# Decoder block on one core: where the first value group is split, and where the weights behind a pair's last cover step are prepared

## The chip, the core and the metric

The kernel runs on one core of a Trainium2 chip. The core has a matrix engine (TensorE, PE in the profile), a vector engine (VectorE, DVE), a scalar engine (ScalarE, ACT), a general one (GpSimd, POOL) and a queue that issues transfers (SyncE, SP). Each engine works through its own list of instructions in order and waits for the others by semaphores. The metric is the device time of one execution in microseconds (us).

## The reference, cut to what matters

The block mixes tokens in two branches, chunked retention and dilated sliding-window attention, merges them with gates and adds an MLP. The change lies in the attention branch and the gate projections beside it:

```python
for gi, (win, dil) in enumerate(ATT_GROUPS):          # 3 groups, 4 heads each
    aq, ak, av = parts[4 + 3 * gi], parts[5 + 3 * gi], parts[6 + 3 * gi]
    o, lse = dilated_group(heads(aq, 4), heads(ak, 4), heads(av, 4), tab, win, dil)
    outs.append(o)
    lses.append(lse)
o_all = jnp.stack(outs, axis=0)
wts = jax.nn.softmax(jnp.stack(lses, axis=0), axis=0)     # weights of the three groups
att = jnp.einsum('gbhs,gbhsd->bshd', wts, o_all).reshape(B, S, ATT_GROUP_W)
att_out = att @ w_att_out
merged = jax.nn.sigmoid(gate_a) * ret_out + jax.nn.sigmoid(gate_b) * att_out
```

Inside `dilated_group` the scores get a bias, a maximum per row, an exponential and a sum; the probabilities then multiply the values.

## The kernel before, in words

**Products in three parts.** Float32 operands are split into a high half (a copy to the rounded type, on ACT) and a low half (a subtraction, on DVE). `mm3` (line 198) makes a product of three matmuls: low weight by high data (L201), high by low (L203), high by high (L205). The products with the values do the same in `pv_mm` (L1399 to L1401), with `pth`/`ptl` the halves of the transposed probabilities and `vh`/`vl` those of the values. A weight's split is `split_w` (L191 on ACT, L192 on DVE).

**Steps.** The program is a list of steps (class `Steps`, line 55), each with loads and a body. A load goes through a ring of three raw tiles on SP's queue (L85): when one is used, the next in the list is issued. For a step that isn't marked `manual` the runner prepares weights of the next one or two steps before its body; a `manual` step gets a function (`ahead`, here `args[0]`) and calls it where it wants the next step's weights prepared, with a bound on how many.

**Attention.** The heads are treated in two pairs (`pair` 0 and 1). Each pair has six attention steps (`att_step`), one for each of three groups and two heads, which project keys and, woven into them, compute the scores of the head before. Then come cover steps (`cover_step`), whose gate projections (8 groups of matmuls, tile `gate`) fill PE while softmax and the products with the values go on:

- The last attention step issues the loads of the first group's values (`v_fetch(pair, 0)`, L1286).
- Cover step 0 weaves in the last scores, then `scores_end` (maximum L1250/L1251 and `ng` L1260 on DVE; eight exponentials, each with its sum, on ACT, L1263), `weights` (the softmax over the groups, L1333 to L1350, with one small exponential L1337 on ACT) and `pscale(0, a)` (L1358 on DVE, L1360 on ACT). At its end ACT takes the gate's sigmoid (L1529), which frees the PSUM bank of the gate; there are two such banks, shared by the gates and the sums of the value products.
- Cover step 1 splits the first group's values, `v_split(pair, 0)`: two copies (L1292, `vh`) and two subtractions (L1293, `vl`).
- Cover step 2 multiplies group 0 (`weave_pv(..., pair, 0)`): transposes (L1375), `pth`/`ptl` (L1379/L1380), products, and `pv_end`, which takes the sum out of PSUM (L1408 on ACT for group 0, L1412 on DVE for the others). Within it the values of group 1 are split, and behind it group 1 is scaled.
- Pair 0 has a cover step 3, which multiplies group 1 and scales group 2 within. Its group 2 is multiplied in the first attention step of pair 1, which also splits that group's values. Pair 1 has cover steps 0 to 2, and its groups 1 and 2 are multiplied in `gate_step`, behind which the output projection (`att_out_step`, tile `ao`) follows.

ACT's and DVE's order is the order of these calls. Cover step 2 is `manual`; cover step 3 and the gate step aren't, so two weight splits (`raw_8615`/`raw_8724` in pair 0, `raw_9954`/`raw_10063` in pair 1) stand at the start of each.

Of the kernel before, what the change touches and what calls it, by code (L numbers as in the profile page):

```python
# [20 lines left out]
NK = D // P  # L21
# [12 lines left out]
COVER = ((0, 1, 2, 3), (4, 5, 6), (9,))  # L34
# [100 lines left out]
def block_kernel(ctx, tc, io, stop=None, dbg=None):  # L135
    nc = tc.nc
    ctx.enter_context(tc.manual_schedule())

    def fv(t):
        return t.bitcast(F32)  # L140
# [44 lines left out]
    steps = Steps(nc, wraw, 3)  # L185
# [300 lines left out]
    def at(gen, n, call):  # L486

        for i, _ in enumerate(gen):
            if i == n:
                call()  # L490
            yield

    def drain(gen):
        for _ in gen:
            pass
# [238 lines left out]
    def wsplit(ap):  # L734
        return ap, split_w
# [373 lines left out]
    for h in range(H):  # L1109
        for c in range(NC):  # L1110
            steps.add((lambda h, c: lambda ahead, *w: chunk(h, c, ahead, *w))(h, c),
                      ([wsplit(io["w_rg"][4 * h + c // 2])] if c % 2 == 0 else []) + [mod_load(later_mods[8 * h + c])],
                      manual=True)


    A = {}
# [14 lines left out]
    def pslice(g, t, blk):  # L1131

        if g == 0:
            return (t[:, 0:128], 1) if blk == 0 else (t[:, 128 + 256 * (blk - 1):128 + 256 * blk], 2)
        if g == 1:
            r, n = blk // 2, blk % 2
            return (t[:, 384 * r:384 * r + 128], 1) if n == 0 else (t[:, 384 * r + 128:384 * r + 384], 2)
        return t[:, 128 * blk:128 * (blk + 1)], 1
# [108 lines left out]
    def scores_end(pair, g, a):  # L1247
        p, t, st = A["p"], A["P", g, a], A["st"]
        if g == 0:
            nc.vector.reduce_max(st[:, g, 0:1, a], t[:, 0:128], axis=AX.X)  # L1250
            nc.vector.reduce_max(st[:, g, 1:8, a], t[:, 128:].rearrange("p (b x) -> p b x", b=7), axis=AX.X)  # L1251
        elif g == 1:
            tv = t.rearrange("p (r x) -> p r x", r=4)
            sv = st[:, g].rearrange("p (r n) x -> p r n x", n=2)
            nc.vector.reduce_max(sv[:, :, 0, a], tv[:, :, 0:128], axis=AX.X)
            nc.vector.reduce_max(sv[:, :, 1, a], tv[:, :, 128:384], axis=AX.X)
        else:
            nc.vector.reduce_max(st[:, g, :, a], t.rearrange("p (b x) -> p b x", b=8), axis=AX.X)
        ng = p.tile([P, 8], F32, tag="ng", bufs=2, name=f"ng{pair}{g}{a}")
        nc.vector.tensor_scalar_mul(ng, st[:, g, :, a], -1.0)  # L1260
        for blk in range(8):
            v = pslice(g, t, blk)[0]
            nc.scalar.activation(v, v, AF.Exp, bias=ng[:, blk:blk + 1], accum_out=st[:, g, blk, 2 + a:3 + a])  # L1263
# [13 lines left out]
    def v_tile(pair, g, j, n):  # L1277
        if g == 0:
            return A["r1"].tile([P, S], F32R, tag="att", bufs=8, name=f"{n}{pair}{g}{j}")
        return ring(f"{n}{pair}{g}{j}")  # L1280
# [4 lines left out]
            lo = A["l", g, j] = v_tile(pair, g, j, "vl")  # L1285
            nc.sync.dma_start(fv(lo).rearrange("p (a b) -> p a b", a=4), v_rows(pair, g, j))  # L1286

    def v_split(pair, g):
        for j in range(2):
            lo = A["l", g, j]  # L1290
            hi = v_tile(pair, g, j, "vh")
            nc.scalar.copy(hi, fv(lo))  # L1292
            nc.vector.tensor_sub(lo, fv(lo), fv(hi))  # L1293
            A["v", g, j] = (hi, lo)

    def vblk(g, blk, a, i):
        j, b = (blk % 2, blk // 2) if g == 1 else (blk // 4, blk % 4)
# [14 lines left out]
    def blocks(t, g):  # L1312

        return t.rearrange("p (r n) x -> p r n x", n=2) if g == 1 else t
# [9 lines left out]
    def weights(pair):  # L1324

        p, st = A["p"], A["st"]
        stn = [st[:, 0], A["stn"][:, 1], A["stn"][:, 2]]
        mx = p.tile([P, 8, 2], F32, tag="mx", name=f"mx{pair}")
        wt = p.tile([P, 3, 8, 2], F32, tag="wt", name=f"wt{pair}")
        pr = p.tile([P, 3, 8, 2], F32, tag="pr", name=f"pr{pair}")  # L1330
        sm = p.tile([P, 8, 2], F32, tag="ssum", name=f"ssum{pair}")
        wg = p.tile([P, 2, 8, 2], F32, tag="wg", name=f"wg{pair}")
        nc.vector.tensor_max(mx, stn[0][:, :, 0:2], stn[1][:, :, 0:2])  # L1333
        nc.vector.tensor_max(mx, mx, stn[2][:, :, 0:2])
        for g in range(3):
            nc.vector.tensor_sub(wt[:, g], stn[g][:, :, 0:2], mx)
        nc.scalar.activation(wt, wt, AF.Exp)  # L1337
        for g in range(3):
            nc.vector.tensor_mul(pr[:, g], wt[:, g], stn[g][:, :, 2:4])
        nc.vector.tensor_add(sm, pr[:, 0], pr[:, 1])  # L1340
        nc.vector.tensor_add(sm, sm, pr[:, 2])
        nc.vector.reciprocal(sm, sm)
        for g in range(3):
            nc.vector.tensor_mul(wt[:, g], wt[:, g], sm)
        A["w", 0] = wt[:, 0]
        ds = [dram.tile([S, 2], F32, name=f"wtd{pair}{g}") for g in (1, 2)]
        for g in (1, 2):
            nc.sync.dma_start(natural(ds[g - 1], 0, 2), wt[:, g])
        for g in (1, 2):
            nc.sync.dma_start(blocks(wg[:, g - 1], g), natural(ds[g - 1], g, 2))  # L1350
            A["w", g] = wg[:, g - 1]

    def pscale(g, a):
        t, w = A["P", g, a], A["w", g]
        for blk in range(8):
            v = pslice(g, t, blk)[0]
            if blk in (0, 2, 4, 5, 7):
                nc.vector.tensor_scalar_mul(v, v, w[:, blk, a:a + 1])  # L1358
            else:
                nc.scalar.mul(v, v, w[:, blk, a:a + 1])  # L1360
        A["scaled", g, a] = True
# [85 lines left out]
    def weave_pv(main, n, pair, *groups):  # L1447


        parts, waits = sum(4 * len(PT[g]) for g in groups), 2 * len(groups) + 1  # L1450
        heavy = max(1.0, (parts - waits) / max(1, n - waits))
        total = parts + waits * (heavy - 1)
        done = share = 0
        for wait in pv(pair, *groups):
            share += heavy if wait else 1
            while done * total < share * n:
                next(main, None)
                done += 1
        drain(main)
# [38 lines left out]
    def cover_step(pair, n):  # L1498


        i = COVER[pair][n]

        def body(*args):
            ps = ps_mm(f"gate0{i}")
            gen = proj_gen(ps, args[-1])
            if n == 0:
                v_fetch(pair, 1)
                weave(gen, 6, scores_gen(pair, *combos[-1]), len(SB[0]), lag=2, rest=False)
                drain(gen)
                scores_end(pair, *combos[-1])  # L1510
                weights(pair)
                for a in range(2):
                    pscale(0, a)
            elif n == 1:
                drain(at(gen, 4, lambda: v_split(pair, 0)))
            elif n == 2:
                v_fetch(pair, 2)

                gen = at(gen, 3, lambda: (args[0](3), v_split(pair, 1)))
                weave_pv(gen, NK - 1, pair, 0)  # L1520
                for a in range(2):
                    pscale(1, a)
            else:
                weave_pv(at(gen, 3, lambda: [pscale(2, a) for a in range(2)]), NK - 1, pair, 1)
            if n > 1:
                t = A["r1"].tile([P, S], F32, tag="att", bufs=8, name=f"g0{i}s")
            else:
                t = ring(f"g0{i}s", F32)
            nc.scalar.activation(t, flat(ps), AF.Sigmoid)  # L1529
            nc.sync.dma_start(gate_d[i], t)  # L1530
        return body

    for pair in range(2):
        for i, (g, a) in enumerate(combos):
            steps.add(att_step(pair, i),
                      [wsplit(io["w_ak"][g * 4 + 2 * pair + a])] +
                      ([(aq_d[pair, *combos[i - 1]], q_prep(pair, *combos[i - 1]))] if i > 0 else []),
                      manual=i == pair == 0)
        for n in range(len(COVER[pair])):
            more = [(aq_d[pair, *combos[-1]], q_prep(pair, *combos[-1]))] if n == 0 else []  # L1540
            steps.add(cover_step(pair, n), more + [wsplit(io["w_gate"][len(COVER[0]) * pair + n])], manual=n == 2)


    G = {}
    gate_ctx = ExitStack()
    mh_ctx = ExitStack()

    def gate_step(w):

        ps = ps_mm("gate9")  # L1550
        gen = at(proj_gen(ps, w), 2, lambda: v_split(1, 2))
        gen = at(gen, 3, lambda: [pscale(2, a) for a in range(2)])
        weave_pv(gen, NK - 1, 1, 1, 2)
        att_ctx.close()
        G["p"] = gate_ctx.enter_context(tc.tile_pool(name="gates", bufs=1, side="right", reuse_waits="tile"))
        t = G["p"].tile([P, S], F32, tag="g1", bufs=8, name="g11")
        nc.scalar.activation(t, flat(ps), AF.Sigmoid)
        G[1, 1] = t
        for j in (0, 2, 3):
            gate_load(1, j)  # L1560
        open_mh()
# [3 lines left out]
        G[b, j] = G["p"].tile([P, S], F32, tag=f"g{b}", bufs=8, name=f"g{b}{j}")  # L1565
        nc.sync.dma_start(G[b, j], gate_d[8 * b + j])

    steps.add(gate_step, [wsplit(io["w_gate"][len(COVER[0] + COVER[1])])])

    def open_mh():  # L1570
        hpool_ctx.close()
# [878 lines left out]
```

## Time and profile before

| what | us |
|---|---|
| median of three runs | 2247.46 |
| lowest and highest run | 2244.88, 2249.23 |
| the profiled execution, its own time | 2244.46 |
| its span, first to last instruction | 2242.7 |
| pair 0: cover step 0 begins on PE | 1061.1 |
| pair 0: cover step 2 / cover step 3 begin on PE | 1087.2 / 1109.0 |
| pair 1: cover step 2 / gate step begin on PE | 1245.6 / 1267.4 |
| output projection begins on PE | 1298.2 |

The mean granted clock of PE is 0.995 of full speed. In the lines of the profile, `L1292 ACT CAST vh<-vl` is a copy by ACT from tile `vl` to tile `vh` at line 1292; a bracket behind a line of the timeline tells how long the engine was idle before it and what released it. `x2` is two such instructions merged. Tile numbers such as `raw_8615l` are the program's own: `h` and `l` behind them are the halves. SPq is SP's queue, where the time is that of issuing and not of the transfer.

### The profile page before, as it was taken

To read this page: it belongs to the slowest core of one execution; us is meant where nothing else is said; L and a number is where in the kernel's file an instruction comes from. 1 tells how busy PE (TensorE), PEld (TensorE's weight loads), DVE (VectorE), ACT (ScalarE), POOL (GpSimd) and SP (SyncE) were. 2 spreads that over 40 slices of the span, in tenths; PEclk is the share of its full clock that TensorE was granted. 3 is DMA by queue.
4 is the path that set the end of the run, shared out by engine and by line. 5 is a ranking of instruction groups with operands and counts; after the bars stand their busy time and mean duration, and the time that the engine had idled before them with its cause. 6 is when DMAs were issued, how large, how long until landed. Compare 5 with 4: busy or idle time off the path is not lost.

```text
span 2242.7 us, 27133 instructions
## 1 busy us (share of the span) xinstructions
PE 2182.0 (97%) x10130; PEld 1804.8 (80%) x10130; DVE 1454.8 (65%) x2285; ACT 908.4 (41%) x1665; POOL 145.4 (6%) x168
## 2 busy tenths in 40 slices
PE   7999999999999999999999999999999999999998
PEld 5887888887877888888888788888777777888887
DVE  6527777754548778855555654677866665787845
ACT  4323333223334445544634633524444444533412
POOL 0001111000011122110000000002000000000003
PEclk9999999999999999999999999999999999999999
DMA  9548999624775556549723365654243344745322
GB/s 362 198 146 279 284 294 277 202 95 178 251 269 167 168 181 208 192 161 247 226 66 97 96 223 180 238 182 153 75 149 138 141 155 148 268 147 169 122 85 76
DMA packets 154371, 408.93 MB, mean 182 GB/s; under 512 B 27062, under 2 KB 54973, under 8 KB 149822
## 3 DMA queue, kind: packets, MB, share of 16 engines
q1 hardware_dynamic: 148542, 363.14, 46.5%
q0 software_dynamic: 5696, 44.04, 8.3%
q8 instruction: 80, 1.31, 0.2%
q14 instruction: 53, 0.43, 0.1%
HBM read 316.27 MB, written 156.13 MB: 211 GB/s over the span
## 4 chain that ended last, share of the span: by engine, by line
PE 44%; DVE 8%; ACT 4%; issue 2%; DMA 1%; POOL 0%; SPq 0%; POOLq 0%; DVEq 0%; ACTq 0%
PE fp L201 2%; PE fp L203 2%; PE fp L205 2%; PE f2a L203 2%; PE f2a L201 2%; PE f2a L205 2%; PE ak L201 2%; PE ak L203 2%; PE ak L205 2%; PE wo L201 1%; PE wo L203 1%; PE wo L205 1%; PE roa L205 1%; PE roa L203 1%; PE roa L201 1%
## 5 line engine op out<-in xcount | busy, mean ns | idle before, releaser
L201 PE MATMUL qap<-hh,qaw 128*128 128x512 f32 x216 | 84.3, 390 | 3.4 <-DVE qat L285 1.7
L205 PE MATMUL qap<-hh,qaw 128*128 128x512 f32 x216 | 84.1, 389 | 0.0
L203 PE MATMUL qap<-hl,qaw 128*128 128x512 f32 x216 | 84.1, 389 | 0.0
L611 POOL TENSOR_TENSOR j<-qk,j 128x512 fp32r<-128x512 f32 x32 | 43.3, 1354 | 469.8 <-ACT j L610 469.8
L1909 ACT ACTIVATE a<-a 128x512 f32<-128x512 f32 x48 | 30.3, 632 | 84.9 <-DVE a L1908 84.9
L1263 ACT ACTIVATE P<-P,ng 128x128 f32<-128x128 f32 (+1 forms) x96 | 41.9, 438 | 39.1 <-DVE ng L1260 39.1
L258 DVE TENSOR_TENSOR fw<-w1r,fw 128x512 fp32r<-128x512 f32 x48 | 32.9, 688 | 37.5 <-ACT fw L248 37.5
L1806 POOL TENSOR_TENSOR accnf<-accnf,sqnf 128x256 f32<-128x256 f32 (+1 forms) x18 | 16.6, 921 | 624.3 <-ACT sqnf L1805 624.3
L2093 ACT CAST w2h<-w2s 128x512 fp32r<-128x512 f32 x36 | 22.4, 621 | 78.0 <-DVE w2s L2131 75.8
L201 PEld LDWEIGHTS qap<-hh,qaw 128*128 128x128 f32 x216 | 40.5, 188 | 12.6 <-DVE qat L285 2.2
L201 PE MATMUL fp<-h2h,fw 128*128 128x512 f32 x128 | 50.0, 390 | 0.0
L633 ACT COPY sm<-sT 128x128 f32<-128x128 f32 x32 | 8.5, 266 | 102.2 <-PE sT L624 100.4
L203 PE MATMUL fp<-h2l,fw 128*128 128x512 f32 x128 | 49.8, 389 | 0.0
L205 PE MATMUL roa<-rh,rwh 128*128 128x512 f32 x128 | 49.8, 389 | 0.0
L203 PE MATMUL roa<-rl,rwh 128*128 128x512 f32 x128 | 49.8, 389 | 0.0
L205 PE MATMUL fp<-h2h,fw 128*128 128x512 f32 x128 | 49.8, 389 | 0.0
L201 PE MATMUL roa<-rh,rwl 128*128 128x512 f32 x128 | 49.8, 389 | 0.0
L1644 DVE TENSOR_TENSOR rwl<-rwl,rwh 128x1024 fp32r<-128x1024 f32 x25 | 30.2, 1220 | 29.1 <-ACT rwh L1674 29.1
L205 PEld LDWEIGHTS qap<-hh,qaw 128*128 128x128 f32 x216 | 40.6, 188 | 8.5
L203 PEld LDWEIGHTS qap<-hl,qaw 128*128 128x128 f32 x216 | 40.5, 188 | 8.3
L1806 POOL TENSOR_TENSOR accn<-accn,sqn 128x512 f32<-128x512 f32 x12 | 15.5, 1294 | 477.9 <-ACT sqn L1805 477.9
L258 DVE TENSOR_TENSOR qaw<-wa,qaw 128x512 fp32r<-128x512 f32 x54 | 36.9, 685 | 8.0 <-ACT qaw L248 8.0
(3081 smaller groups left out, 7187.1 us busy)
## 6 DMA issues: line engine op xcount, KB each, us to landing
v<-vd SPq DMA_DIRECT2D x32, 512.0 KB, 5.1
raw<-in_w_ada_dram SPq DMA_DIRECT2D x32, 512.0 KB, 4.9
w1r<-in_w_ff_dram SPq DMA_DIRECT2D x32, 512.0 KB, 5.0
vd<-vo SPq DMA_DIRECT2D x24, 512.0 KB, 6.4
yt<-y POOLq DMA_DIRECT2D x6, 2048.0 KB, 15.3
xsd<-as SPq DMA_DIRECT2D x24, 512.0 KB, 2.7
w2r<-in_w_ff2s_dram SPq DMA_DIRECT2D x24, 512.0 KB, 7.6
em<-in_w_ada_dram SPq DMA_DIRECT2D x16, 512.0 KB, 10.2
```

The source lines that it names most:

```text
L201: nc.tensor.matmul(o, wl, xh, start=first, stop=False, skip_group_check=skip)
L203: nc.tensor.matmul(o, wh, xl, start=False, stop=False, skip_group_check=skip)
L205: nc.tensor.matmul(o, wh, xh, start=False, stop=last, skip_group_check=skip)
L258: nc.vector.tensor_sub(t[:, 512:], src, fv(t[:, :512]))
L611: nc.gpsimd.tensor_sub(t[:, 1], src, fv(t[:, 0]))
L633: nc.scalar.copy(sm, ps[:, :C])
L1263: nc.scalar.activation(v, v, AF.Exp, bias=ng[:, blk:blk + 1], accum_out=st[:, g, blk, 2 + a:3 + a])
L1644: nc.vector.tensor_sub(lo, fv(lo), fv(hi))
L1806: (nc.vector if f == 7 else nc.gpsimd).tensor_add(G["acc", key], G["acc", key], sq)
L1909: nc.scalar.activation(o, o, AF.Relu)
L2093: nc.scalar.copy(hi, src)
```

## The change

`v_split` gets a switch that leaves the low halves out, and `v_low_part` makes one of them. The copies of group 0 now stand in cover step 0, behind the last matmul's work and ahead of `scores_end`; the subtractions stand in `weights`, between the small exponential and the products behind it. Cover step 1 has only its projection left. The cover steps from 2 on and the gate step become `manual`: cover step 3 of pair 0 and the gate step call `ahead(2)` after the fourth projection group, ahead of scaling group 2, and the second weight split moves to the start of the step that follows. No instruction is added or removed; PE's list stays as it is.

```diff
-    def v_split(pair, g):
+    def v_split(pair, g, low=True):
         for j in range(2):
             lo = A["l", g, j]
             hi = v_tile(pair, g, j, "vh")
             nc.scalar.copy(hi, fv(lo))
-            nc.vector.tensor_sub(lo, fv(lo), fv(hi))
             A["v", g, j] = (hi, lo)
+            if low:
+                v_low_part(g, j)
+
+    def v_low_part(g, j):
+        hi, lo = A["v", g, j]
+        nc.vector.tensor_sub(lo, fv(lo), fv(hi))
...
         nc.scalar.activation(wt, wt, AF.Exp)
+
+        for j in range(2):
+            v_low_part(0, j)
         for g in range(3):
             nc.vector.tensor_mul(pr[:, g], wt[:, g], stn[g][:, :, 2:4])
...
                 drain(gen)
+                v_split(pair, 0, False)
                 scores_end(pair, *combos[-1])
                 weights(pair)
                 for a in range(2):
                     pscale(0, a)
             elif n == 1:
-                drain(at(gen, 4, lambda: v_split(pair, 0)))
+                drain(gen)
...
             else:
-                weave_pv(at(gen, 3, lambda: [pscale(2, a) for a in range(2)]), NK - 1, pair, 1)
+
+                gen = at(gen, 3, lambda: (args[0](2), [pscale(2, a) for a in range(2)]))
+                weave_pv(gen, NK - 1, pair, 1)
...
-            steps.add(cover_step(pair, n), more + [wsplit(io["w_gate"][len(COVER[0]) * pair + n])], manual=n == 2)
+            steps.add(cover_step(pair, n), more + [wsplit(io["w_gate"][len(COVER[0]) * pair + n])], manual=n > 1)
...
-    def gate_step(w):
+    def gate_step(ahead, w):
 
         ps = ps_mm("gate9")
         gen = at(proj_gen(ps, w), 2, lambda: v_split(1, 2))
-        gen = at(gen, 3, lambda: [pscale(2, a) for a in range(2)])
+        gen = at(gen, 3, lambda: (ahead(2), [pscale(2, a) for a in range(2)]))
...
-    steps.add(gate_step, [wsplit(io["w_gate"][len(COVER[0] + COVER[1])])])
+    steps.add(gate_step, [wsplit(io["w_gate"][len(COVER[0] + COVER[1])])], manual=True)
```

## Prediction, made before the changed kernel ran

> **What bounds the kernel now.** I read the page first, then the list of waits of TensorE (PE) over the attention stage, then the timelines of ACT, DVE, PE and the DMA queue around the two places that the change touches. Engine times are us from the start of the span.
>
> ```profile
> span 2242.7 us, 27133 instructions
> PE 2182.0 (97%) x10130; PEld 1804.8 (80%) x10130; DVE 1454.8 (65%) x2285; ACT 908.4 (41%) x1665; POOL 145.4 (6%) x168
> ```
>
> PE is busy for 97% of the span, and the change leaves PE's instructions and their order alone. So it can only shorten or lengthen PE's pauses. In the list of waits (who waited for whom: us in total, times, longest) those of this stage, 1060 to 1302, are few:
>
> ```profile
> PE pv L1399 <- DVE P L1412: 3.3, 4, 0.9
> PE pv L1400 <- DVE ptl110(0, 0, 0)_10497 L1380: 1.2, 1, 1.2
> PE pv L1400 <- DVE ptl010(0, 0, 0)_9158 L1380: 1.2, 1, 1.2
> PE gate L201 <- ACT g00s L1529: 0.8, 1, 0.8
> PE pv L1399 <- DVE vl L1293: 0.7, 1, 0.7
> ```
>
> The `ptl010`/`ptl110` waits are at the start of the last cover step and of the gate step, one per pair; the `g00s` wait is where cover step 2 waits for a PSUM bank; the others are for a bank that DVE empties (L1412) and for values (`vl`). All that can be won is of this size.
>
> **Part 1: the first group's values.** Two ACT copies (`vh`) and two DVE subtractions (`vl`) leave cover step 1. ACT in both pairs (pair 0 first; the last row is pair 1) and DVE in pair 0:
>
> ```profile
> 1069.81 1.03 ACT L191 CAST raw_8603h<-raw 128x1024 fp32r<-128x1024 f32 x1
> ...
> 1076.91 0.40 ACT L1263 ACTIVATE P<-P,ng 128x128 f32<-128x128 f32 x1 [6.07 <-DVE ng L1260]
> ...
> 1087.97 2.00 ACT L1292 CAST vh<-vl 128x1024 fp32r<-128x1024 f32 x2
> ...
> 1235.32 0.40 ACT L1263 ACTIVATE P<-P,ng 128x128 f32<-128x128 f32 x1 [6.07 <-DVE ng L1260]
> ```
>
> ```profile
> 1081.01 0.18 DVE L1339 TENSOR_TENSOR pr<-wt,st 128x16 f32<-128x16 f32 x1 [3.47 <-ACT wt L1337]
> ...
> 1089.24 2.35 DVE L1293 TENSOR_TENSOR vl<-vl,vh 128x1024 fp32r<-128x1024 f32 x2
> ```
>
> The copies move from 1087.97 into ACT's idle 6.07 us ahead of the exponentials, the subtractions into DVE's idle 3.47 us behind the last `wt` difference. By length both fit: 2.00 in 6.07, 2.35 in 3.47.
>
> *What it wins.* PE at the first product of cover step 2:
>
> ```profile
> 1085.80 0.60 PE L1375 MATMUL pt000(0, 0, 0)_8939<-ct,P 128*128 128x128 f32 x4
> 1087.19 0.73 PE L201 MATMUL gate<-hh,raw_8603l 128*128 128x512 f32 x2 [0.79 <-ACT g00s L1529]
> ...
> 1090.48 0.62 PE L205 MATMUL gate<-hh,raw_8603h 128*128 128x512 f32 x2
> ...
> 1092.47 0.28 PE L1401 MATMUL pv<-pth000(0, 0, 0)_8944,vh 128*128 128x256 f32 x1
> ...
> 1094.20 0.62 PE L205 MATMUL gate<-hh,raw_8603h 128*128 128x512 f32 x2
> ...
> 1094.89 0.28 PE L1401 MATMUL pv<-pth000(2, 1, 2)_8959,vh 128*128 128x256 f32 x1
> ```
>
> From the gate's last matmul to the third of a product's trio are 1092.47 - 1090.48 = 1.99 us where it waits, and 1094.89 - 1094.20 = 0.69 where it doesn't. With 2 us off ACT and 2.35 off DVE in front of `pth000` and `ptl000` both are ready in time, so 1.30 us are won. I take it for each pair: -2.60. It can't be more; 0 if something else holds them.
>
> *What it costs.* ACT takes its queue in order, so a copy that waits for its values holds the 16 exponentials, `wt`, the scaling, `g00s` and with it the gate's PSUM bank behind it, and PE waits for `g00s` already (0.79), so nothing covers a delay. When do the values land? They are issued in the attention step before, right behind a weight load, on the same queue. From the DMA queue's timeline, the DMA issues of 1066 to 1069 (KB each, us to landing) and of 1217.5 to 1219, and a table by windows (last columns: granted clock, DMA share, GB/s):
>
> ```profile
> 1066.78 0.37 SPq L85 DMA_DIRECT2D raw<-in_w_ak_dram  x1
> 1067.20 1.27 SPq L1286 DMA_DIRECT2D vl<-vad  x2
> ...
> 1217.94 0.37 SPq L85 DMA_DIRECT2D raw<-in_w_att_out_dram  x1
> ```
>
> ```profile
> vl<-vad SPq DMA_DIRECT2D x2, 512.0 KB
> raw<-in_w_ak_dram SPq DMA_DIRECT2D x1, 512.0 KB, 11.2
> ```
>
> ```profile
> raw<-in_w_att_out_dram SPq DMA_DIRECT2D x1, 512.0 KB, 5.9
> ```
>
> ```profile
> 1078.00:1081.50 3.50, 3.50 (x18) 2.88 (x17) 0.47 (x4) 2.98 (x13) 1.15 (x1) 1.00 1.04 358
> ```
>
> In pair 0 the weight load ahead of the values lands at 1066.78 + 11.2 = 1078.0. Behind it 512 KB at 358 GB/s take 1.46 us: the two value tiles land near 1079.4 and 1080.9. The second copy (1.0) then ends near 1081.9, where the exponentials began at 1076.91: **+5.0 us**, on the path. Before, nobody asked for these values until 1087.97, which is why no row shows a wait for them. In pair 1 the load ahead of them, issued at 1217.94, lands after 5.9 us; counted the same way the values are there near 1226.8, over 8 us before the exponentials at 1235.32: 0 there. Bounds for pair 0: 0, if the load took 5.9 as in pair 1 (values at 1075.6, copies done by 1076.6), and 8, if they land 3 us later still.
>
> **Part 2: weights within the last cover step.** In the last cover step before, two weight splits (`raw_8615`, `raw_8724`) stand ahead of the first `ptl`. Now the first is taken after the fourth of the eight projection groups, ahead of the scaling of group 2, and the second goes to the start of the next step. Pair 1 has the same in the gate step and the first output step.
>
> ```profile
> 1112.03 0.63 PE L205 MATMUL gate<-hh,raw_8609h 128*128 128x512 f32 x2
> ...
> 1114.30 0.28 PE L1401 MATMUL pv<-pth010(0, 0, 0)_9157,vh 128*128 128x256 f32 x1
> ...
> 1123.16 0.36 PE L1399 MATMUL pv<-pth011(0, 0, 0)_9220,vl 128*128 128x256 f32 x1 [0.73 <-DVE P L1412]
> ```
>
> ```profile
> 1112.33 1.22 DVE L192 TENSOR_TENSOR raw_8724l<-raw,raw_8724h 128x1024 fp32r<-128x1024 f32 x1
> ...
> 1118.62 2.04 DVE L1358 TENSOR_SCALAR P<-P,wg 128x128 f32<-128x128 f32 x10
> ...
> 1135.56 2.35 DVE L1293 TENSOR_TENSOR vl<-vl,vh 128x1024 fp32r<-128x1024 f32 x2
> ...
> 1281.32 2.07 DVE L1358 TENSOR_SCALAR P<-P,wg 128x128 f32<-128x128 f32 x10
> ```
>
> ```profile
> 1118.01 1.87 ACT L1360 ACTIVATE P<-P,wg 128x128 f32<-128x128 f32 x6
> ```
>
> *Won at the start:* 1114.30 - 1112.03 - 0.69 = 1.58 us, in each pair.
>
> *Lost in pair 0, last cover step:* the ACT half (1.03) goes in at 1118.01, its DVE half (1.22) can begin at 1119.04 and ends at 1120.26, where the scaling began at 1118.62: 1.6 later. The same DVE queue then empties the bank (L1412) that PE waits for at 1123.16, without slack: +1.6. The two cancel.
>
> *Lost in the next attention step, pair 0:* there the `vl` subtractions already hold PE (0.7 in the list of waits), behind the query's and a weight's split on DVE. `raw_8724` goes in front of them: +1.1 (its 1.22, less the overlap of neighbours on DVE, about 0.1).
>
> *Pair 1, gate step:* the split lies ahead of the scaling at 1281.32, where DVE runs without a gap; the two transposes, the `ptl` and L1412 behind it, which PE takes up at once, move by the same 1.1: -1.58 + 1.1 = -0.5. `raw_10063` moves to the first output step, where DVE and ACT have gaps and PE needs it a step later: 0. Two DMAs are issued later on SP's queue (a query tile behind the gate's output, a weight of `w_o` behind the gate loads); both are read a step or more later: 0, at worst one load's 1.46.
>
> Bounds of part 2: -3.2, if the late splits cost nothing, to +3, if nothing is won at the start.
>
> **The clock.** The stall makes PE's pause about 5.8 us (0.79 + 5.0). What follows a pause is in the list of waits and the windows (first number the length, then PE busy; the clock is third from the end):
>
> ```profile
> PE rg L201 <- DVE kl L644: 4.7, 1, 4.7
> PE fp L201 <- DVE ft2h2t L285: 3.5, 1, 3.5
> PE fp L203 <- DVE xt L1947: 2.5, 3, 1.1
> ```
>
> ```profile
> 664.32:671.14 6.82, 4.86 (x11) 3.85 (x12) 1.35 (x4) 0.71 (x3) 0.00 (x0) 0.50 1.07 397
> ...
> 1609.81:1613.22 3.41, 3.41 (x10) 2.64 (x9) 3.38 (x6) 1.24 (x2) 0.00 (x0) 0.50 0.00 0
> 1647.35:1650.77 3.42, 2.94 (x7) 2.36 (x8) 2.12 (x4) 2.20 (x5) 0.00 (x0) 0.50 0.01 2
> ```
>
> After the pause of 4.7 PE worked 4.86 us at half clock, after that of 3.5 it worked 2.94: 2.43 and 1.47 us lost. I take the mean, **+1.95**, with 0 and 2.43 as bounds. One doubt: the transposes `pt000` need the scaled blocks, so they too wait and split the pause into some 2 and 3.7 us. But at 1609.81 the clock fell after pauses of only 1.1 each, so a split pause suffices.
>
> The Trainium skill, "TensorE: Matmul & The Clock Gate", section on the HAM clock gate, says that the clock halves after an idle window of about 3.4 us on a free-running raster. By that, as an estimate, a 3.7 us pause would hold a whole window only about once in twelve times, and the sum would mostly lack the 1.95; the row at 1609.81 speaks against so strict a reading.
>
> **The sum:** 5.0 - 2.6 (part 1) - 1.6 + 1.6 + 1.1 - 0.5 (part 2) + 1.95 = **+5.0** against the profiled 2244.46, so 2249.4. That execution lies 3.0 under the median of the runs, 2247.46, so I forecast **2252.4** for the median.
>
> **Rivals.**
> 1. *The values land in time in pair 0* (not slower). Place: the ACT copies ahead of the exponentials. For it: pair 1's 5.9 us. Against: the 11.2 of the load ahead. No stall and no clock loss: 5.0 - 5.0 - 1.95 = -2.0, 2245.5. The point is the second tile's landing: past 1075.9 each us costs one, and the 2.0 won is gone at 1077.9.
> 2. *Stall, but no drop of the clock*: +3.0, 2250.5. For it: the split of the pause; against it the row at 1609.81.
> 3. *The late splits are free*: gaps absorb them, +5.0 - 1.6 - 1.1 - 1.1 = +1.2, 2248.7; with rival 1 it is the best there is, about -5.8, 2241.7. Against: DVE has no gap before either place.
> 4. *A longer stall*: the values land 3 us later, 2255.4. For it: DMA was at 358 GB/s and full throughout; against: nothing upstream changes.
>
> **How the numbers follow.** Forecast 0.58, rival 1 0.15, rival 2 0.10, rival 3 0.07 (half of it with rival 1), rival 4 0.10. A change under 0.2% (4.5 us) can't be told from none here. Slower by more: five sixths of the forecast, all of rival 4 and a little of rival 2, 0.62. Faster by more: rival 3 with rival 1 and a tail of rival 1, 0.08. The rest, 0.30, is within. The range 2245.5 to 2257 leaves rival 1's lower half, the best case and the top of rival 4 out, some 2 in 10; the forecast's own is 2250 to 2255.
>
> **What will show it.** Right: in pair 0 ACT idle ahead of `vh`, ended by a DMA of `vl`; exponentials near 1082; the wait for `g00s` at some 5.8 us in pair 0 and 0.8 in pair 1; clock 0.5 right behind; waits for `ptl010` and `ptl110` gone; the first L1412 wait of pair 0 up by 1.6 and the `vl` wait up by 1.1. Wrong: exponentials at 1077, or a shorter L1412 wait. If PE's waits of the stage sum to less than before, the forecast is wrong in sign.

## The result, and the profile after

The changed kernel takes 2254.8 us (median), the kernel before, run beside it, 2247.6: a ratio of 1.0037, with an interval of 1.0027 to 1.0048. It is slower by 7.2 us by the medians; the ratio, which is worked out over all runs and not from the medians, makes it 8.3. The profiled execution took 2256.17 us (before: 2244.46), with a span of 2254.3 and a mean granted clock of 0.992 (before: 0.995). These two profiles lie 11.7 us apart, since the one of before is faster than its median by 3.2 us and this one slower by 1.4; what follows shows places and mechanisms, and their sizes in one execution. The page shows that time was lost, not where:

```profile
span 2254.3 us, 27133 instructions
PE 2186.9 (97%) x10130; PEld 1808.9 (80%) x10130; DVE 1456.1 (65%) x2285; ACT 909.1 (40%) x1665; POOL 145.4 (6%) x168
```

PE has the same 10130 instructions and is busy for 4.9 us longer. Part of the loss is therefore not waiting but slower work. In PE's list of waits over the attention stage (us in total, times, longest) stand, after:

```profile
PE pv L1407 <- DVE P L1420: 4.9, 4, 2.3
PE gate L201 <- ACT g00s L1540: 3.8, 1, 3.8
PE pt000(0, 0, 0)_8939 L1383 <- DVE P L1366: 3.4, 1, 3.4
PE pv L1407 <- DVE vl L1299: 1.8, 1, 1.8
```

Lines have moved by 6 to 11: L1407 was L1399, L1420 was L1412, L1540 was L1529. The waits for `ptl010` and `ptl110` are gone (1.2 each). Waits are new or longer in three places of pair 0: `pt000` and `g00s`, 7.2 us together where 0.8 stood; one of the L1420 waits, 2.3 where the longest was 0.9; and `vl`, 1.8 where 0.7 stood. ACT's timeline of pair 0 shows where the first of them comes from:

```profile
1072.24 1.03 ACT L191 CAST raw_8603h<-raw 128x1024 fp32r<-128x1024 f32 x1
...
1081.17 1.05 ACT L1292 CAST vh<-vl 128x1024 fp32r<-128x1024 f32 x1 [7.90 <-DMA vl<-vad]
1083.89 1.05 ACT L1292 CAST vh<-vl 128x1024 fp32r<-128x1024 f32 x1 [1.67 <-DMA vl<-vad]
1084.85 0.40 ACT L1263 ACTIVATE P<-P,ng 128x128 f32<-128x128 f32 x1
```

ACT stands idle ahead of each copy, and a value transfer ends each wait. Before, the bracket ahead of the exponentials named the maximum (`ng`). PE's timeline shows what the waits in the other two places are:

```profile
1131.25 0.36 PE L1407 MATMUL pv<-pth011(0, 0, 0)_9208,vl 128*128 128x256 f32 x1 [2.32 <-DVE P L1420]
1147.59 0.33 PE L1407 MATMUL pv<-pth020(0, 0, 0)_9354,vl 128*128 128x128 f32 x1 [1.82 <-DVE vl L1299]
```

And a table by windows of those places of this stage where the clock was granted at half (length, then PE's busy time; the clock is third from the end):

```profile
1091.36:1098.19 6.83, 3.09 (x8) 2.40 (x9) 3.34 (x8) 6.00 (x9) 0.00 (x0) 0.50 0.90 115
1132.32:1135.73 3.41, 3.41 (x14) 2.82 (x12) 0.04 (x1) 0.48 (x1) 0.00 (x0) 0.50 0.00 0
1149.38:1152.79 3.41, 3.41 (x12) 2.74 (x11) 0.49 (x1) 0.42 (x1) 0.00 (x0) 0.50 0.77 266
1159.62:1163.03 3.41, 3.41 (x13) 3.02 (x13) 2.05 (x2) 0.00 (x0) 0.00 (x0) 0.50 0.00 0
```

The profile of before has no such stretch between 1060 and 1300. Here are four, with 13.32 us of PE work at half speed, so about 6.7 us of it lost.

To see what each place costs, compare when the first product of each step starts on PE. PE's list is the same in all kernels of the table, so the difference grows where time is lost and shrinks where it is won. In us, after minus before, each kernel's profiled execution on its own clock (a difference that stands already at cover step 0 comes from further up; up to 4.5 us of it stand there in kernels whose code up to there is that of before, so it isn't put down to the change):

| first product of | before at | whole change | part 1 alone | part 2 alone | pair 1's parts | all gains | gains kept |
|---|---|---|---|---|---|---|---|
| cover step 0, pair 0 | 1061.07 | 1.25 | 1.82 | 0.74 | 2.82 | 2.84 | 4.52 |
| cover step 2, pair 0 | 1087.19 | 7.92 | 6.85 | 0.75 | 2.85 | 6.79 | 4.53 |
| cover step 3, pair 0 | 1108.96 | 8.07 | 7.03 | 0.76 | 2.89 | 5.49 | 4.58 |
| first attention step, pair 1 | 1130.83 | 9.63 | 7.01 | 2.34 | 2.88 | 4.25 | 3.30 |
| second attention step, pair 1 | 1150.79 | 13.93 | 7.00 | 3.49 | 2.88 | 3.25 | 2.28 |
| cover step 2, pair 1 | 1245.61 | 13.96 | 7.02 | 3.51 | 2.88 | 3.26 | 2.30 |
| gate step | 1267.38 | 12.67 | 5.71 | 3.53 | 1.59 | 2.00 | 1.04 |
| output projection | 1298.20 | 12.22 | 5.71 | 3.10 | 1.12 | 0.44 | 1.04 |

The columns behind the whole change are the experiments below. Read down a column: each step between two rows is one place.

### The profile page after: what moved, and what is told of

It reads as the page before. It is cut to its first block, busy times and chain, and to the rows that moved or that the text cites. A ratio compares the mean times of both kernels' runs of the same rounds, so it can differ in the third digit from the quotient of the medians.

```text
span 2254.3 us, 27133 instructions
## 1 busy us (share of the span) xinstructions
PE 2186.9 (97%) x10130; PEld 1808.9 (80%) x10130; DVE 1456.1 (65%) x2285; ACT 909.1 (40%) x1665; POOL 145.4 (6%) x168
## 3 DMA queue, kind: packets, MB, share of 16 engines
q8 instruction: 80, 1.31, 0.2%
## 4 chain that ended last, share of the span: by engine, by line
PE 42%; DVE 7%; ACT 3%; DMA 3%; issue 1%; SPq 0%; POOL 0%; POOLq 0%; DVEq 0%; ACTq 0%
PE fp L201 2%; PE fp L203 2%; PE fp L205 2%; PE f2a L203 2%; PE f2a L205 2%; PE f2a L201 2%; PE ak L201 1%; PE ak L203 1%; PE ak L205 1%; PE wo L201 1%; PE wo L205 1%; PE wo L203 1%; PE roa L205 1%; PE roa L203 1%; PE roa L201 1%
## 5 line engine op out<-in xcount | busy, mean ns | idle before, releaser
L201 PEld LDWEIGHTS qap<-hh,qaw 128*128 128x128 f32 x216 | 40.9, 190 | 11.7 <-ACT qat L280 2.5
L633 ACT COPY sm<-sT 128x128 f32<-128x128 f32 x32 | 8.5, 265 | 102.3 <-PE sT L624 100.2
## 6 DMA issues: line engine op xcount, KB each, us to landing
em<-in_w_ada_dram SPq DMA_DIRECT2D x16, 512.0 KB, 10.2
```

Of the source, the lines that this page charges most:

```text
L201: nc.tensor.matmul(o, wl, xh, start=first, stop=False, skip_group_check=skip)
L633: nc.scalar.copy(sm, ps[:, :C])
```

## The experiments

**Part 1 alone.** Everything of part 2 undone:

```diff
-                gen = at(gen, 3, lambda: (args[0](2), [pscale(2, a) for a in range(2)]))
-                weave_pv(gen, NK - 1, pair, 1)
+                weave_pv(at(gen, 3, lambda: [pscale(2, a) for a in range(2)]), NK - 1, pair, 1)
...
-            steps.add(cover_step(pair, n), more + [...], manual=n > 1)
+            steps.add(cover_step(pair, n), more + [...], manual=n == 2)
...
-    steps.add(gate_step, [wsplit(...)], manual=True)
+    steps.add(gate_step, [wsplit(...)])
```

> Part 1 alone, both pairs; the weight splits as before. Theory (pair 0's ACT copies wait for late values, PE's clock halves behind the pause): exponentials of pair 0 near 1083 to 1085, the wait for g00s and the transposes some 6 to 8 us together, one drop of the clock behind it, 1.3 won in each pair, nothing else moved: +4 to +6.5, 2251.5 to 2254. Rival (the loss is part 2's): at least 2.6 faster, 2245.

Measured: 2251.9 us where the kernel before had 2246.7, a ratio of 1.0019 (1.0010 to 1.0028). ACT's timeline:

```profile
1081.33 1.05 ACT L1292 CAST vh<-vl 128x1024 fp32r<-128x1024 f32 x1 [8.32 <-DMA vl<-vad]
1082.82 1.05 ACT L1292 CAST vh<-vl 128x1024 fp32r<-128x1024 f32 x1 [0.43 <-DMA vl<-vad]
1083.77 0.40 ACT L1263 ACTIVATE P<-P,ng 128x128 f32<-128x128 f32 x1
```

PE waits 1.8 us for `pt000` and 3.8 for `g00s` here. The second tile comes 1.5 us behind the first, 2.7 in the whole change's profile. By the table the stall is 6.85 - 1.82 = 5.03, against 7.92 - 1.25 = 6.67 there; the difference is that later tile (1.2 us) and a first tile that is 0.4 later. Cover step 2 then adds 0.18 instead of giving back 1.30, and a table by windows has the reason, the clock at half:

```profile
1090.32:1097.15 6.83, 3.11 (x8) 2.43 (x9) 3.32 (x8) 5.97 (x9) 0.00 (x0) 0.50 0.91 140
```

Pair 1 gives back 1.31, and nothing moves between. So part 1 alone brings the first loss and none of the later ones.

This profile also bears on what holds the values up. From the table of DMA issues the weight load ahead of them on SP's queue (512 KB, 5.4 us from issue to landing); then the shares of the engines' time of POOL's queue (q0) and SP's (q1) over 1075 to 1078, and of SP's over 1078 to 1081:

```profile
raw<-in_w_ak_dram SPq DMA_DIRECT2D x1, 512.0 KB, 5.4
```

```profile
q0 software_dynamic: 16, 1.05, 93.4%
q1 hardware_dynamic: 17, 0.02, 1.6%
```

```profile
q1 hardware_dynamic: 914, 0.95, 99.0%
```

That load was issued at 1067.89 and so landed at 1073.3, yet the first copy could not start before 1081.33, 8.0 us later. In between a transfer of POOL's (`yt`, issued at 1068.89) had the engines almost to itself over 1075 to 1078. So the values didn't come right behind the load ahead of them; by these rows they came behind POOL's transfer. No run moved that transfer, so its part is read from the rows and not tested.

**Part 2 alone.** The kernel before with part 2's lines only.

> Part 2 alone. Theory: 1.6 won at ptl010 and ptl110, first L1412 wait of pair 0 near 2.3, vl wait of the next step near 1.8, gate step 0.45 shorter: +0.7 without drops of the clock; the two longer waits bring the clock down once to three times at 1.6 each, so 2249 to 2253. Rival (drops of the clock come from the stall alone): within 1 of before, no drop between 1100 and 1170.

Measured: 2248.8 us, a ratio of 1.0007 (0.9998 to 1.0016): by its time alone it can't be told from the kernel before. The medians lie 2.1 us apart. Its profile has the two longer waits of the whole change, 2.3 and 1.8 us, and the waits for `ptl010` and `ptl110` are gone. The step-by-step table says what they cost: +1.58 in cover step 3, +1.15 in the first attention step, -0.43 in the gate step. The prediction had 0, +1.1 and -0.5. The odd one is cover step 3, where the clock fell once (at 1125.53, for 3.41 us); the wait for `vl` cost its 1.1 and brought no half clock. In the whole change's profile the same two places cost 1.56 and 4.30, with three drops. The same wait thus drew the clock down in one profile and not in the other; a later section takes this up.

**The values one attention step earlier.** If late values are the cause, loading them earlier should cure it. The loads go from the last attention step of the pair to the one before:

```diff
-            if i == len(combos) - 1:
+            if i == len(combos) - 2:
                 v_fetch(pair, 0)
```

> The whole change, but the first group's values are loaded one attention step earlier. Theory (late values are the stall): ACT idle before vh gone or under 1, exponentials of pair 0 near 1077, wait for g00s 0.8 again, no drop near 1091; part 2's share stays: 2247 to 2251, some 5 to 7 under the changed kernel. Rival (the copies or the order themselves stall, or the load is as late wherever it is issued): like the changed kernel, 2254.

Measured: 2259.8 us, a ratio of 1.0051 (1.0038 to 1.0065). Slower still, where 2247 to 2251 was expected. The values were there in time, but ACT then stood in front of something else:

```profile
1082.33 1.05 ACT L191 CAST raw_8607h<-raw 128x1024 fp32r<-128x1024 f32 x1 [10.20 <-DMA raw<-in_w_gate_dram]
1083.28 2.00 ACT L1292 CAST vh<-vl 128x1024 fp32r<-128x1024 f32 x2
...
1089.45 0.40 ACT L1263 ACTIVATE P<-P,ng 128x128 f32<-128x128 f32 x1 [4.17 <-DVE ng L1260]
```

SP's queue tells why (the time is that of issuing):

```profile
1049.19 4.37 SPq L1286 DMA_DIRECT2D vl<-vad  x2
1056.60 0.33 SPq L1326 DMA_DIRECT2D std<-st  x1
1071.33 0.36 SPq L1327 DMA_DIRECT2D stn<-std  x1
1071.80 7.68 SPq L85 DMA_DIRECT2D raw<-in_w_gate_dram  x2
```

A statistic is written to memory (`std`) and read back (`stn`), and the read waits for the write. From one to the other are 14.73 us here. In the kernel before, the same two lines stand at 1054.36 and 1064.91, 10.55 apart:

```profile
1054.36 0.33 SPq L1321 DMA_DIRECT2D std<-st  x1
1064.91 0.38 SPq L1322 DMA_DIRECT2D stn<-std  x1
1065.38 1.30 SPq L85 DMA_DIRECT2D raw<-in_w_gate_dram  x2
```

SP takes its queue in order, so the gate's weight loads behind that read are issued at 1071.80 instead of 1065.38 (4.2 us later when the two clocks are laid together at cover step 0), and the first of them lands only at 1082.31. ACT now waits for a weight where it waited for values. DVE's half of that weight (L192 at 1083.41) then stands ahead of the last scores, so the maximum comes late too, and PE waits 7.0 us for `pt000` and 3.4 for `g00s`. Moving the loads moved the wait to the next transfer.

**The values in the second attention step.** Four attention steps earlier than in the kernel before, where the queue is less crowded (`if i == 1:`).

> The whole change, with the first group's values loaded in each pair's second attention step (tiles landed some 50 us ahead of the copies, and out of the way of the weight loads around 1066 to 1080). Theory: no wait of ACT ahead of vh, exponentials of pair 0 at 1077, g00s waited for 0.8, no drop of the clock near 1091; part 1 wins its 1.3 in each pair, part 2 gives +0.7 and up to three drops of the clock at 1.6: 2245 to 2250. Rival (the stall is not about when the values land): 2253 or more.

Measured: 2250.4 us, a ratio of 1.0013 (1.0002 to 1.0025), with all of the change's other parts in it. About half of the change's loss is gone (3.7 us by the medians are left of 7.2). ACT no longer waits for values, but one step further up a gate weight is late now, 3.3 us where the whole change waits 1.4 and the kernel before not at all:

```profile
1062.86 1.05 ACT L191 CAST raw_8505h<-raw 128x1024 fp32r<-128x1024 f32 x1 [3.27 <-DMA raw<-in_w_gate_dram]
1063.81 1.00 ACT L1209 CAST kh<-ak 128x1024 fp32r<-128x1024 f32 x1
```

The key halves `kh` stand behind that weight in ACT's queue, and PE waits 0.9 us for `kl` and 2.3 for `g00s`. Expected were 0.8 us for `g00s` and no half clock near 1091; the clock fell at 1092.84. Early loads are not free in either place that was tried.

**Pair 1 alone.** Part 1 in pair 1 only, where the prediction has the values land 8 us ahead, and of part 2 only the gate step:

```diff
+                if pair:
+                    v_split(pair, 0, False)
...
-                drain(gen)
+                drain(gen if pair else at(gen, 4, lambda: v_split(pair, 0)))
```

> Part 1 in pair 1 alone, part 2 in the gate step alone; pair 0 as before. Theory: only gains are left, 1.3 and 0.45: 2245.8, and no new drop of the clock. Rival (the gains are not there either): 2247.6 or more.

Measured: 2244.8 us, a ratio of 0.9991 (0.9982 to 1.0000), so by its time alone at the edge of what can be told from the kernel before. The table: nothing until cover step 2 of pair 1, there -1.29, in the gate step -0.47. These are the two gains of the prediction, -1.30 and -0.5, without any of the losses.

**Pauses filled.** To test whether half clock follows from PE's pauses, part 1 alone got spare products on PE, whose results nobody uses: 7 ahead of the first transposes of cover step 2 and 14 behind them; then, in a second kernel, 18 and 7.

```diff
+                    def spare_mm(n):
+                        for _ in range(n):
+                            nc.tensor.matmul(spare, args[-1][0][:, :P], hh[0][:, :512], start=True, stop=True)
...
+                    spare_mm(7)
+                    gen = spare_then(gen)
```

> Part 1 alone, with 21 spare matmuls on PE while it waits for g00s in pair 0 (7 ahead of the first transposes, 14 behind them; they take some 4.8 us of the wait and write a bank that nobody reads). Theory (the drop of the clock is the pause's): same start of cover step 2 as in part 1 alone, no clock of 0.5 there, and cover step 2 1.3 shorter than before instead of 0.2 longer. Rival (the clock drops whatever PE does, or the loss behind the stall is not the clock's): cover step 2 as long as in part 1 alone.

The first of the two (2253.7 us, a single run) left a pause of 2.58 us, and the clock fell behind it all the same, against the expectation, but onto the spare products:

```profile
1092.20 0.69 PE L1383 MATMUL pt000(0, 0, 0)_8947<-ct,P 128*128 128x128 f32 x4 [2.58 <-DVE P L1366]
1092.65 5.06 PE L1534 MATMUL spare<-hh,raw_8603h 128*128 128x512 f32 x14
1097.54 0.62 PE L201 MATMUL gate<-hh,raw_8603l 128*128 128x512 f32 x2
...
1117.90 0.71 PE L201 MATMUL gate<-hh,raw_8609l 128*128 128x512 f32 x2
```

That gave a clean reading of cover step 2 at full clock: 1117.90 - 1097.54 = 20.36 us. The kernel before takes 21.77 (1087.19 to 1108.96), part 1 alone 21.95. So part 1 does win 1.41 us there, and half clock takes 1.59 of it back.

> Part 1 alone, with spare products on PE in the two pauses of pair 0 (18 ahead of the first transposes of cover step 2, 7 behind them; their results are not used). Theory (the half clock behind the late values follows PE's pauses): no stretch at clock 0.5 begins between 1085 and 1105, and the first gate product of cover step 2 to that of cover step 3 takes 20.4 us, as in e6 behind its spare products, where part 1 alone took 21.95 and the kernel before 21.77; the first product of cover step 2 stands where it stands in part 1 alone, within 0.5 us, since the sigmoid that it waits for is bound by the values. Rival (the clock falls there whatever PE does, or the exponentials' own work draws it down): a stretch at 0.5 of 3.4 us or more begins between 1088 and 1096 all the same, and the step takes 21.4 to 22.

The second (2254.8 us, a single run) has no stretch at half clock in the stage. Windows from the first spare products to the first gate products, and PE's timeline:

```profile
1088.00:1093.33 5.33, 5.26 (x26) 4.10 (x25) 2.48 (x14) 4.03 (x17) 0.00 (x0) 1.00 1.01 212
1093.33:1097.37 4.04, 1.88 (x11) 1.22 (x9) 1.71 (x7) 4.01 (x8) 0.00 (x0) 1.00 0.88 152
1097.37:1102.00 4.63, 4.63 (x28) 4.06 (x29) 3.11 (x4) 3.26 (x5) 0.00 (x0) 1.00 0.27 15
```

```profile
1097.37 0.73 PE L201 MATMUL gate<-hh,raw_8603l 128*128 128x512 f32 x2 [2.16 <-ACT g00s L1551]
...
1117.84 0.71 PE L201 MATMUL gate<-hh,raw_8609l 128*128 128x512 f32 x2
```

The step took 20.47 us, as forecast for full clock. One half of the expectation missed: the step was to begin where it begins in part 1 alone, and it began later, at 1097.37. The spare products don't explain that, since the first gate product waits for `g00s` and not for them: the values themselves landed later, as ACT shows:

```profile
1084.66 1.05 ACT L1292 CAST vh<-vl 128x1024 fp32r<-128x1024 f32 x1 [11.05 <-DMA vl<-vad]
```

From the issue of the loads (1069.62) to this copy are 15.0 us, 12.9 in part 1 alone. So this kernel isn't faster, although its clock is cured.

**Part 2 with the split later.** The weight split was in front of the scaling; now it stands behind it, after the seventh projection group in cover step 3 and the sixth in the gate step. Part 1 isn't in it.

```diff
-at(gen, 3, lambda: (args[0](2), [pscale(2, a) for a in range(2)]))
+at(at(gen, 3, lambda: [pscale(2, a) for a in range(2)]), 6, lambda: args[0](2))
```

> Part 2 alone, but the split within the last cover step is called after the seventh projection group instead of the fourth, in the gate step after the sixth. Theory (DVE's order delays L1412 and the scaling): first L1412 wait of pair 0 back to 0.7, so cover step 3 1.6 shorter than before; vl wait of the next step still 1.8 (+1.1); gate step 1.6 shorter: -2.1, 2244.7, with no drop of the clock in cover step 3. Rival (the place within the step does not matter): like part 2 alone, 2248.8.

Measured: 2248.7 us, a ratio of 1.0003 (0.9991 to 1.0015). The steps themselves came as meant: the L1412 wait is back at 0.9 or less, cover step 3 is 1.28 shorter than before and the gate step 1.56. But more than that was given back in the attention step between, in the wait for `vl`, which was expected at 1.8:

```profile
PE pv L1399 <- DVE P L1412: 3.4, 4, 0.9
PE pv L1399 <- DVE vl L1293: 3.1, 1, 3.1
```

ACT's timeline shows what got in front of the values: a weight (`raw_9319`) whose load was late.

```profile
1135.73 1.05 ACT L191 CAST raw_9319h<-raw 128x1024 fp32r<-128x1024 f32 x1 [1.83 <-DMA raw<-in_w_ak_dram]
...
1137.16 1.99 ACT L1292 CAST vh<-vl 128x1024 fp32r<-128x1024 f32 x2
```

A weight's raw tile comes free only when it has been split, so a later split means a later load. SP's queue, first in this kernel and then in the kernel before:

```profile
1131.32 0.35 SPq L85 DMA_DIRECT2D raw<-in_w_ak_dram  x1
```

```profile
1112.44 0.34 SPq L85 DMA_DIRECT2D raw<-in_w_ak_dram  x1
```

The attention step lost 7.2 us: 2.4 of it is the longer wait, and nearly all of the rest two stretches at half clock behind it (10.2 us long together, PE busy throughout, so some 5 us lost).

**All gains together, with the early values.** The whole change, values loaded in the second attention step, the split late in both places, and in pair 1's first attention step the next weight split moved behind the values, by making that step `manual`:

```diff
-weave_pv(at(gen, 0, lambda: v_split(0, 2)), NK - 1, 0, 2)
+weave_pv(at(at(gen, 0, lambda: v_split(0, 2)), 3, lambda: args[0](2)), NK - 1, 0, 2)
```

> All that the theory says can be won: values in the second attention step, part 1 in both pairs, the later splits of the run before, and in pair 1's first attention step the next weight and query prepared after its fourth group instead of ahead of the values' split. Theory: -2.6 (part 1) -1.6 (cover step 3) -0.9 (vl wait) -1.6 (gate step) = -6.7, 2240. Rival (gains of one place come back as waits of the next): 2244 or more.

Measured: 2243.4 us, a ratio of 0.9983 (0.9969 to 0.9998): faster than the changed kernel and than the kernel before, than that by 3.3 us only, where 6.7 was expected. By the table every gain is there from cover step 2 of pair 0 on: -1.30, -1.24, -1.00, -1.26, and in the gate step -1.56. Ahead of it stands +3.95: PE waits 2.2 us for `kl` and 2.3 for `g00s` (0.8 before), as in the kernel that loads the values in the second attention step, and put down to the early loads again.

**Gains kept, without the early loads.** The same, with part 1 in pair 1 only and the values loaded where they were.

> All that the runs so far showed to win, without the early loads that cost 2.4 us in e8: the split ahead of the exponentials in pair 1 alone, the weight split of cover step 3 at that step's sixth place, of the gate step at its fifth, and of pair 1's first attention step within the last step of pair 0's attention. Theory (each of these gains stands by itself, and the rest of pair 0's stretch is the kernel before): cover step 3 about -1.2, the attention step behind it -1.0, pair 1's cover step 2 -1.3, gate step -1.4, by the steps of e8, together -4.9: about 2241.8 where the kernel before has 2246.7, and not over 2244; no half-clock stretch and no new wait over 1 us between 1060 and 1320. Rival (part of what e8 won came from its early value loads, which moved later transfers forward): about 2244.5, as in e4, with waits of 1 us or more left at L1420 or for vl in pair 0.

Measured: 2243.3 us where the kernel before had 2246.0, a ratio of 0.9983 (0.9974 to 0.9992). It is faster than the kernel before by 2.7 us, though not by the 4.9 expected. The first three steps came: -1.28, -1.02, -1.26. The gate step came out at 0, since the clock fell in it, at 1294.57 for 3.41 us; no half clock was expected. No wait over 0.9 us is left in the stage, so this drop came without a long wait. By the medians the kernel gains about as much as the one with all gains, with less moved.

## Why the prediction was right, and where its terms were off

The forecast was 2252.4 by a stall in pair 0 against small gains; the measurement is 2254.8, slower as forecast, by the stall forecast. That it is only 2.4 us off owes something to luck, as the terms show. Here they are against the table:

| term | forecast | whole change | single part |
|---|---|---|---|
| stall ahead of cover step 2, pair 0 | +5.0 | +6.67 | +5.03 |
| cover step 2, pair 0: gain and clock | -1.30 + 1.95 | +0.15 | +0.18 |
| cover step 3, pair 0 | 0 | +1.56 | +1.58 |
| first attention step, pair 1 | +1.1 | +4.30 | +1.15 |
| cover step 2, pair 1 | -1.30 | -1.29 | -1.31 |
| gate step | -0.5 | -0.45 | -0.43 |

- *The stall: right in place and size, its reason in part.* Part 1 alone has exponentials at 1083.77 - 1.82 = 1081.95 on the clock of before, where 1081.9 was forecast. An agreement to 0.05 us is luck, for the same stall is 1.6 us longer in the whole change's profile. The prediction reckoned the landing from the load ahead of the values (11.2 us) and 1.46 for each tile. In the whole change's profile that holds in the main: the load takes 12.2 and lands at 1079.75, the first copy starts at 1081.17. In part 1 alone that load took 5.4 us, the very condition of rival 1 (5.9 as in pair 1), and the stall came all the same, behind POOL's transfer. So rival 1 fell, but not because the load is slow: the 11.2 us were the mark of a busy stretch and not the cause, which the prediction doesn't name.
- *The wait's split: right in sum for part 1 alone.* It was forecast as one wait for `g00s` of 5.8; it is two, 1.8 for `pt000` and 3.8 for `g00s` in part 1 alone (3.4 and 3.8 in the whole change), since the transposes wait for the scaled blocks as the doubt in the prediction said.
- *The gains: right,* -1.41 at full clock in pair 0 and -1.29 in pair 1 where -1.30 was forecast for each. The half clock hides the first.
- *DVE's queue: right.* In the whole change the wait at L1420 rose from 0.73 to 2.32 us, by the 1.6 forecast, that for `vl` from 0.7 to 1.8, by 1.1, and the gate step gave -0.45. Rival 3, in which gaps absorb the split, fell.
- *The clock: the term that was mis-sized.* The prediction gave one drop to the long stall, 1.95, and none to the two shorter waits that it had itself forecast to 0.1 us. The long stall's drop cost 1.45 to 1.59. The shorter waits, 2.3 and 1.8 us, were followed by three more drops in the whole change's profile and by one in part 2's, each worth about 1.6. So its sentence that the change can only shorten or lengthen PE's pauses was too narrow as well: PE's work was slower by some 6.7 us in that profile.

So the sum of the prediction lacks a part of the clock's loss at L1420 and `vl`. How much of it on the median can't be read from single profiles. By the medians part 1 alone cost 5.2 us (4.35 by the prediction's terms) and part 2 alone 2.1 (0.6 by its terms), together 7.3, where the whole change has 7.2. By the ratios they are 4.3, 1.6 and 8.3, and each interval reaches about 2 us either way. So the parts may add up, or something may be lost only where both are there; these runs can't tell.

**What decides whether the clock falls.** The stretches at half clock of one profile all begin on a raster of 3.413 us: in the whole change's, 1132.32 - 1091.36 is 12 steps of it, 1149.38 - 1132.32 is 5, 1159.62 - 1149.38 is 3. The windows of this raster just ahead of the four drops:

```profile
1087.95:1091.36 3.41, 0.69 (x4) 0.45 (x4) 2.31 (x14) 2.10 (x8) 0.00 (x0) 1.00 1.05 221
1128.91:1132.32 3.41, 1.09 (x9) 1.06 (x9) 2.65 (x3) 0.48 (x1) 0.00 (x0) 1.00 0.27 106
1145.97:1149.38 3.41, 1.79 (x14) 1.76 (x15) 3.41 (x5) 1.54 (x3) 0.00 (x0) 1.00 0.91 294
1156.21:1159.62 3.41, 2.52 (x21) 2.12 (x20) 2.30 (x2) 1.05 (x1) 0.00 (x0) 1.00 0.03 5
```

In three of them PE was busy for 0.69, 1.09 and 1.79 of 3.41 us. The fourth holds 2.52 and only a wait of 0.9 us at L1420, as the kernel before has too. Part 2 alone has the same wait of 1.82 us for `vl`, ended at 1140.29, and no drop. On its raster that wait lies across two windows, ahead of and behind 1139.18:

```profile
1122.12:1125.53 3.41, 1.60 (x10) 1.50 (x11) 2.12 (x2) 0.00 (x0) 0.00 (x0) 1.00 0.10 38
1135.77:1139.18 3.41, 2.69 (x14) 1.89 (x12) 3.41 (x5) 3.41 (x6) 0.00 (x0) 1.00 0.63 198
1139.18:1142.60 3.42, 2.31 (x16) 2.19 (x17) 3.39 (x4) 1.04 (x3) 0.00 (x0) 1.00 0.87 296
```

Neither half leaves PE busy for less than 2.3 us, and the clock stays; the first row, with 1.60, is the one ahead of its drop. Counted over the profiles of this study from 100 to 2200 us, with PE's busy time as the profile models it: all 41 full-clock windows with PE busy for under 42.5% were followed by half clock; of 38 between 42.5% and 53%, 9 were; of 7232 above that, 5, the fourth row above among them. Those 5 are not explained. In all five windows PE ran through short products (128 columns), which start 0.11 us apart while each is booked with 0.27, so the modelled ends may count too much there; no run tested it. The limits of 42.5% and 53% were chosen with these counts in view.

By this count, as an estimate: a wait of length w in otherwise full work empties a window past half (1.7 us) only if at least 1.7 of it falls into one window. Where it falls is chance: about (3.41 - w + 2 (w - 1.7)) / 3.41 of all positions, 0.68 for 2.3 us and 0.53 for 1.8. At 1.6 us a drop this is 1.9 us for the two waits. That is an upper figure, for of the 38 windows with PE busy between 42.5% and 53% most, 29, were not followed by half clock. With the sure limit, PE idle for 57.5% or 1.96 us, the same reckoning gives about 0.53 for 2.3 us, none for 1.8, and 0.8 us in all. So the forecast would have been some 5.8 to 6.9 us above the kernel before, against 7.2 by the medians. That estimate was made after the result; no run tested it by itself.

The Trainium skill, "TensorE: Matmul & The Clock Gate", section on the HAM clock gate, gives a free-running window of 3413 ns, which these traces bear out, and has the clock halve after an idle window. Here it halved after windows in which PE worked for up to half of the time, so a wait of two microseconds can be enough.

## What to carry to other kernels

Moving work in front of something urgent on an in-order engine makes its inputs urgent too: before moving a copy up, look up when its transfer lands, behind what stands ahead of it on its queue and beside what the other queues move then, and not only whether the engine has a gap of the right length. Moving the transfer up as well passed the wait on in both places tried here, to the weights behind it on the queue; of this change the parts were worth keeping whose inputs had long been there. On PE a new wait of about 2 us or more can cost twice, once for itself and once, with some chance, for the half clock behind it (about 1.6 us here).

## What the hardware showed that was not expected

- The clock fell behind windows in which PE was far from idle: with PE busy for 0.69 to 1.79 of 3.41 us in three of the four rows above.
- Filling a pause with products that nobody uses keeps the clock up: in one profile each, cover step 2 took 20.47 us behind filled pauses and 21.95 without.
- How long the values take to land differs between profiles by 2 us, more than the 1.3 that part 1 wins in a pair. From issue to the first copy's start are 13.1 us in the whole change (1068.09 to 1081.17), 12.9 in part 1 alone (1068.40 to 1081.33) and 15.0 in the kernel with 18 and 7 spare products (1069.62 to 1084.66). POOL's queue issues its transfer within 1.1 us behind, and the two queues take turns here: in the whole change POOL's has 87.0% of the engines' time over 1074 to 1077, with 2.6% for SP's, and SP's 100.2% over 1080 to 1083 (counted by the packets that start there). The weight load ahead of the values landed ahead of POOL's turn in part 1 alone (5.4 us) and behind it in the other two (12.2 and 12.9); what decides that was not tried.
